# A weave that counts two more microseconds for each transfer, paces its reloads, and keeps two output weights on the chip

## The chip, the cores and the metric

The kernel runs on one core of a Trainium2 chip. The time is device time in microseconds (us), lower is better; three runs of the kernel before gave 2216.96, 2217.48 and 2220.29 us, a median of 2217.48.

## The reference

One inference step of a two-layer encoder for two groups of frames, 1024 of a prompt and 32 of a sample, 1024 wide, all in fp32. Cut to what matters:

```python
# layer 0: mLSTM mixer (8 heads, chunks of 64), layer 1: windowed attention (16 query heads, 2 kv heads)
mix = mlstm_mixer(x, w_in_a, b_gate_a, g_norm_a, w_out_a, C0, n0, m0)            # layer 0
x = layer_norm(ALPHA * x + mix, ln_g[0, 0], ln_b[0, 0])
x = layer_norm(ALPHA * x + swiglu(x, w_gu[0], w_down[0]), ln_g[0, 1], ln_b[0, 1])
k, v = split(x @ w_kv)
mix = sink_attention(x @ w_q_b, window(k), window(v), sinks, alibi) @ w_out_b    # layer 1
x = layer_norm(ALPHA * x + mix, ln_g[1, 0], ln_b[1, 0])
x = layer_norm(ALPHA * x + swiglu(x, w_gu[1], w_down[1]), ln_g[1, 1], ln_b[1, 1])
```

Outputs are x, the mLSTM states and the last key and value rows.

## The kernel before

**Tiling.** The 1056 frames of both groups are the columns of one activation ACT of 128 partitions by 8 tiles by 1056. A dense product is made of three fp32r matmuls (lines 677 to 679): the activation is held as a rounded high part and a low rest (SX), and so is each weight (tile w, two halves of 512 columns each). A weight read from its input goes through a raw tile wr: ScalarE makes the high part (line 429), VectorE or GpSimd the low part (line 443). ffn() uses a Strassen-like scheme of seven products; its intermediate results go out to DRAM (hs) and come back.

**Stages, by the time in the trace.** Projections and the mLSTM (0 to about 300 us; its small steps are woven between the projections' matmuls), output projection and norm (to 520), the first FFN (to 1205), the projections to k, v and q, attention and two quarters of its output projection (to 1450), the last two quarters woven with the norm (to 1560), the second FFN.

**Weights used more than once.** wkv, w_q_b and w_out_b serve three times each, since the frames come in three groups. The first time a weight is split it is written to DRAM in both parts, and later uses load the split halves (line 425, 512 KB each) from there. split_early() does this splitting ahead of its time, in quarters, beside the mLSTM: a quarter comes in to the tile area (line 1338), ScalarE casts it in place (line 1340), VectorE or GpSimd takes the rest (line 1342), and it goes out (line 1344). It ends when the flag early["over"] is set; what it has not reached is split at its first use.

**What sets the order.** The program is written out by a planner, Weave, while it is built. Each side task is a generator that yields At(engine, reads, writes): the engine of its next step and what that step needs. A Clock follows each instruction with estimated durations and keeps for each cell of each tile the time at which it is ready. Before and within each dense product, tick() places every side step whose estimated start has come. So the estimate decides only where a step stands in the queue of its engine; at run time every engine takes its queue in order, and a step whose operand has not landed holds all steps behind it. A transfer's end is estimated from a chain of all transfers, pipe, and 0.7 us.

**Halves.** Weights holds at most five halves in tiles w (SLOTS = 5). Its feed() asks for the next half as soon as a slot is free, or straight into a place given in home: the Mixer that opens after attention gives the tile E (ex in the trace) as home to weights 2 to 7 of the last use of w_out_b.

**The end of attention.** PLAN asks for the output tiles of the first quarters (g = 0 and g = 1) of w_out_b's eight weights among the q projections; late_out() then makes the last two quarters, g = 2 and g = 3, weights 0 to 7 in order, and reports each finished tile to norm_tail(), whose norms of the first quarters run meanwhile.

Of the kernel before, what the change touches and what calls it, by code (L numbers as in the profile page):

```python
# [19 lines left out]
KT = D // P  # L20
# [44 lines left out]
class Clock:  # L65
# [7 lines left out]
    def __init__(self, nc):  # L73
        self.nc = nc
        self.free = dict.fromkeys(self.LAG, 0.0)
        self.tiles, self.base = {}, {}
        self.lock, self.holder = 0.0, None
        self.pipe = 0.0
        self.window, self.busy, self.slow = -1, 0.0, True
        nc.push_inst_callback(self.see)  # L80

# [31 lines left out]
    def time(self, reads=(), writes=()):  # L113
# [6 lines left out]
                t = max(t, float(x[kinds, half, cells].max()))  # L120
        return t

    def begin(self, e, at):

        held = self.lock if self.holder != e else 0.0
        return max(self.free[e], at, held)
# [9 lines left out]
    def see(self, i, *_):  # L136
        e = str(i.engine).split(".")[-1]
        op = i.opcode
        if e not in self.free or op in ("EventSemaphore", "Drain", "UnconditionalBranch"):
            return  # L140
        aps = lambda l: [a for a in l if hasattr(a, "bass_ap")]
        inner = lambda l: [a for a in l if not a.bass_ap.tensor.name.startswith(("in_", "out_"))]
        ins, outs = aps(i.ins), aps(i.outs)
        if not outs and op != "LoadActFuncSet":
            return
        at = self.time(inner(ins), inner(outs))
        own = self.free[e] + 0.163 if e == "PE" else 0.0
        start = self.free[e] if at <= own else max(self.free[e], at + self.LAG[e])
        size = lambda a: int(np.prod([c for _, c in a.ap[1:]]))
        if op == "DMACopy":  # L150
            n, row = 4, min(a.ap[-1][1] * 4 for a in (*ins, *outs))
            for _, c in outs[0].ap:
                n *= c
            rate = 0.39 if row >= 2048 else 0.30 if row >= 1024 else 0.2 if row >= 512 else 0.1 if row > 4 else 8.5e-5
            self.pipe = max(start + 1.3, self.pipe) + n / rate / 1e6
            self.free[e] = start + 0.4
            end = self.pipe + 0.7
        elif e == "PE":
            end = self.matmul(i, start, size(ins[0])) + 0.163
        else:  # L160
            d = self.cost(i, e, op, ins, outs, size) / 1e3
            if len(outs) > 1 and e == "DVE":
                d += 0.08
            if e in ("DVE", "Pool") and self.shared(e, op, i, ins, outs):
                if self.holder not in (None, e):
                    start = max(start, self.lock)
                self.lock, self.holder = start + d, e
            end = start + d
            part = outs and outs[0].ap[0][1] in (HEADS, 64)
            self.free[e] = end + (0.014 if part else -self.LAP.get(e, 0.0))  # L170
        for l, kind in ((ins, 1), (outs, 0)):
            for a in inner(l):
                x, half, cells = self.part(a.bass_ap, a.ap)
                x[kind, half, cells] = end
# [45 lines left out]
class At:  # L220
# [7 lines left out]
    def start(self, clk):  # L228
        if self.time is None:
            if self.when and not self.when():  # L230
                return None
            reads = self.reads() if callable(self.reads) else self.reads
            self.time = clk.time(reads, self.writes)
        t = self.time
        for ring in self.room:
            if not ring.open():
                return None
            t = max(t, ring.time(clk))
        if t:
            t += clk.LAG.get(self.engine, 0.034)  # L240
        if self.engine is None:
            return t
        if self.engine == "EITHER":
            return min(clk.begin(e, t) for e in ("DVE", "Pool"))
        if self.engine == "SP":
            return max(t, clk.free["SP"], clk.pipe - 1.0)
        return t if self.engine == "PE" else max(t, clk.free[self.engine])
# [87 lines left out]
class Weights:  # L335
# [151 lines left out]
    def start(self, clk):  # L487
        if not (self.ahead and self._ready()):
            return None
        key = self.jobs[self.njob]  # L490
        t = clk.whole(self.raw[key[0]]) if key[0] in self.raw else 0.0
        if key in self.home:
            t = max(t, clk.time((), (self.home[key],)))
        else:
            t = max(t, self.new.ring("w").time(clk))
        return max(t + clk.LAG[self.engine], clk.free[self.engine])

    @property
# [17 lines left out]
def kernel(ctx: ExitStack, tc: tile.TileContext, A, O):  # L516
    nc = tc.nc
    ctx.enter_context(tc.manual_schedule())
    clk = Clock(nc)
# [38 lines left out]
    def add(name, idx):  # L558
        units.append(A[name][idx] if idx is not None else A[name])
        return len(units) - 1  # L560
# [19 lines left out]
    def again(name, m):  # L580

        u = add(name, m)
        if (name, m) in split:
            halves[u] = split[name, m]
        else:
            split[name, m] = kept[u] = dram.tile([P, 2, 2, D // 2], F32, name=f"{name}_{m}")
            first[name, m] = u
        return u
# [30 lines left out]
    U_B = {}  # L619
    for kind, m, g in PLAN:  # L620
        name, m0 = {"q": ("wqb", m), "k": ("wkv", 0), "v": ("wkv", 1), "o": ("wout_b", m)}[kind]
        U_B[kind, m, g] = again(name, m0)
    U_OUT_B = [again("wout_b", u) for u in range(8)]
    add_ffn(1)
    on_vector.update((u, 1) for u in U_OUT_A)
    on_vector.update((u, f) for u in U_Q[:1] + U_KV + [U_B['q', 0, 0]] for f in range(2))
# [5 lines left out]
    W = Weights(nc, clk, new_weight, units, pairs, on_vector, kept, halves, wv)  # L632
# [824 lines left out]
    lx = Mixer(ea.close, U_OUT_A[:6])  # L1457
# [429 lines left out]
    eb = ExitStack()  # L1887
# [244 lines left out]
    for kind, m, g in PLAN:  # L2132
        u = U_B[kind, m, g]
        if kind == "q":
            wv.until(lambda: ast["scored"] >= 3 * (done - 3))
            q_group(m, g)
            done += 1
        elif kind == "o":
            wv.until(lambda: ast["split"] > g and (not g or ast["scored"] >= min(53 + 3 * m, 72)))
            outs.append(out_tile(u, m, g, True))  # L2140
            W.done(u)
        else:
            for t in (1, 2):
                (k_group if kind == "k" else v_group)(u, t)
                if kind == "v":
                    wv.launch(v_turn(t))
            W.done(u)
            if kind == "v":
                v_parts(9, cv[:], P)
                k_part(ck, SEQ, P)  # L2150
                nc.sync.dma_start(O["p_k"], kout[:, :P])
                nc.sync.dma_start(O["s_k"], kout[:, P:])
                nc.sync.dma_start(O["p_v"], vT[2][:, 128:256])
                nc.sync.dma_start(O["s_v"], vT[2][:, 256:])
    wv.drain(task)
    wv.drain(parts)
    for t in outs:
        wv.drain(t)
    lx = Mixer(eb.close, U_OUT_B[2:])

    def late_out(g, cols, after):
        for m in range(KT):
            if g > 1:
                out_tile(U_OUT_B[m], m, g)
                if g == 3:
                    W.done(U_OUT_B[m])
            after(range(KT), m)

    tasks = norm_tail(2, late_out, [lx])
    ffn(1, 3, tasks, lx, True)  # L2170
# [127 lines left out]
```

## Time and profile before

| | us |
|---|---|
| median of three runs | 2217.48 |
| profiled execution, whole | 2219.07 |
| its span | 2217.3 |
| TensorE (PE) busy in it | 2182.8 |

Of the profiled execution 1.8 us lie around its span, and it is 1.6 us over the median of the three runs. Times in the trace count from the start of the span. "Idle" is time in which an engine does nothing that the profile shows; a releaser is whatever ended it. SPq stands for the DMA issues of SyncE.

### The profile page before, as it was taken

The page shows a single profiled execution, that of the slowest core. Times are in us where ns is not written, and L with a number is a line of the kernel's source. Part 1 is how long each engine was busy: PE and PEld are TensorE (multiplying, and loading weights), DVE is VectorE, ACT ScalarE, POOL GpSimd, SP SyncE. Part 2 cuts the span into 40 slices and gives each one's busy share as a digit, 9 for nine tenths or more (in the row PEclk, how much of TensorE's full clock was granted, in tenths as well). Part 3 has the DMA queues.
Part 4 walks back from the last instruction along what each step waited for, and adds up shares of the span by engine and source line. Part 5 has one row for each costly group of instructions (what it writes and reads, how often), then busy time and mean ns, then how long its engine had stood idle before and what let it go on. Part 6 is the DMA issues. An engine that isn't in the chain of part 4 may idle for free.

```text
span 2217.3 us, 44432 instructions
## 1 busy us (share of the span) xinstructions
PE 2182.8 (98%) x17116; PEld 2150.9 (97%) x17116; DVE 1512.6 (68%) x3030; ACT 1021.9 (46%) x2308; POOL 800.0 (36%) x805
## 2 busy tenths in 40 slices
PE   9999999999999999999999999999999999999997
PEld 9989999999999999999999999989999999999997
DVE  5566566777766566476677887778675665566677
ACT  4554454555434444321245877657443443421234
POOL 1343300001544545444401565500454554544510
PEclk9999999999999999999999999999999999999999
DMA  4455522302434424598516568761344344489712
GB/s 154 143 155 174 185 81 74 118 30 77 170 123 173 148 107 165 188 309 283 174 66 223 175 194 267 233 212 58 117 166 146 128 155 145 135 290 322 244 52 78
DMA packets 218052, 356.69 MB, mean 161 GB/s; under 512 B 18608, under 2 KB 151016, under 8 KB 217840
## 3 DMA queue, kind: packets, MB, share of 16 engines
q1 hardware_dynamic: 212800, 348.54, 47.0%
q10 hardware_dynamic: 5040, 5.31, 0.7%
q8 instruction: 135, 2.21, 0.4%
q14 instruction: 77, 0.63, 0.1%
HBM read 251.96 MB, written 101.82 MB: 160 GB/s over the span
## 4 chain that ended last, share of the span: by engine, by line
PE 85%; DVE 5%; DMA 4%; ACT 3%; issue 1%; SPq 1%; POOL 1%; ACTq 0%; DVEq 0%; POOLq 0%
PE d L677 10%; PE d L678 10%; PE d L679 10%; PE A L677 9%; PE A L679 9%; PE A L678 9%; PE B L677 7%; PE B L678 7%; PE B L679 7%; PE T L2068 1%; PE O L2085 1%; PE psS L2049 1%; PE O L2084 1%; PE psS L2050 1%; DMA wr<-in_dn 1%
## 5 line engine op out<-in xcount | busy, mean ns | idle before, releaser
L443 POOL TENSOR_TENSOR w<-wr,w 128x512 fp32r<-128x512 f32 x395 | 561.5, 1437 | 796.2 <-ACT w L429 793.5
L429 ACT CAST w<-wr 128x512 fp32r<-128x512 f32 (+1 forms) x478 | 290.3, 617 | 454.6 <-DVE wr L390 262.7
L677 PE MATMUL A<-sx,w 128*128 128x264 f32 x1280 | 364.1, 284 | 4.2 <-ACT z L1706 3.7
L679 PE MATMUL A<-sx,w 128*128 128x264 f32 x1280 | 363.4, 284 | 0.0
L678 PE MATMUL A<-sx,w 128*128 128x264 f32 x1280 | 363.1, 284 | 0.0
L677 PE MATMUL d<-sx,w 128*128 128x264 f32 (+2 forms) x1092 | 339.5, 311 | 3.3 <-DMA w<-wout_b 2.8
L678 PE MATMUL d<-sx,w 128*128 128x264 f32 (+2 forms) x1092 | 329.5, 302 | 1.5 <-DVE sx L800 1.5
L679 PE MATMUL d<-sx,w 128*128 128x264 f32 (+2 forms) x1092 | 329.3, 302 | 0.0
L677 PEld LDWEIGHTS A<-sx,w 128*128 128x128 f32 x1280 | 240.4, 188 | 5.1 <-ACT z L1706 4.1
L679 PEld LDWEIGHTS A<-sx,w 128*128 128x128 f32 x1280 | 241.2, 188 | 0.0
L678 PEld LDWEIGHTS A<-sx,w 128*128 128x128 f32 x1280 | 240.8, 188 | 0.0
L677 PE MATMUL B<-ex,w 128*128 128x264 f32 x832 | 236.6, 284 | 0.0
L679 PE MATMUL B<-ex,w 128*128 128x264 f32 x832 | 235.9, 284 | 0.0
L678 PE MATMUL B<-ex,w 128*128 128x264 f32 x832 | 235.9, 284 | 0.0
L677 PEld LDWEIGHTS d<-sx,w 128*128 128x128 f32 x1092 | 205.5, 188 | 5.3 <-DMA w<-wout_b 3.0
L678 PEld LDWEIGHTS d<-sx,w 128*128 128x128 f32 x1092 | 205.8, 188 | 2.6 <-DVE sx L800 2.1
L679 PEld LDWEIGHTS d<-sx,w 128*128 128x128 f32 x1092 | 205.4, 188 | 0.0
L677 PE MATMUL d<-sx,ex 128*128 128x264 f32 x552 | 160.3, 290 | 0.0
L1572 DVE TENSOR_TENSOR z<-z 128x528 fp32r<-128x528 f32 x136 | 110.3, 824 | 72.8 <-ACT z L1570 72.5
L679 PE MATMUL d<-sx,ex 128*128 128x264 f32 x552 | 156.7, 284 | 1.1 <-DVE ex L443 1.1
L679 PEld LDWEIGHTS B<-ex,w 128*128 128x128 f32 x832 | 156.8, 188 | 0.0
L678 PE MATMUL d<-sx,ex 128*128 128x264 f32 x552 | 156.7, 284 | 0.0
(303 smaller groups left out, 5858.2 us busy)
## 6 DMA issues: line engine op xcount, KB each, us to landing
wr<-in_gu SPq DMA_DIRECT2D x96, 512.0 KB, 4.8
hs_x<-z SPq DMA_DIRECT2D x72, 528.0 KB, 3.1
hs_t<-z SPq DMA_DIRECT2D x64, 528.0 KB, 3.5
sx<-hs_x SPq DMA_DIRECT2D x112, 264.0 KB, 5.6
w<-wqb SPq DMA_DIRECT2D x48, 512.0 KB, 4.4
sx<-hs_t SPq DMA_DIRECT2D x64, 264.0 KB, 6.0
ex<-hs_t SPq DMA_DIRECT2D x64, 264.0 KB, 6.0
w<-wout_b SPq DMA_DIRECT2D x33, 512.0 KB, 4.3
```

The costliest lines, as they stand in the source:

```text
L429: self.nc.scalar.copy(hi, r)
L443: eng.tensor_sub(lo, r, hi.bitcast(F32))
L677: nc.tensor.matmul(out, ah, bh, start=start and k == 0, stop=False, **kw)
L678: nc.tensor.matmul(out, ah, bl, start=False, stop=False, **kw)
L679: nc.tensor.matmul(out, al, bh, start=False, stop=stop and k == last, **kw)
L1572: clk.sooner(2 * N4, hi).tensor_sub(lo.bitcast(F32R), buf(s), hi)
L2049: nc.tensor.matmul(psS[h][:R, lo:256], q[:, h, tk], KH[g2][:, kc], start=True, stop=False)
L2050: nc.tensor.matmul(psS[h][:R, lo:256], q[:, h, tk], KL[g2][:, kc], start=False, stop=True)
L2068: nc.tensor.transpose(pt[:nk, i, h, :R], p[:R, h, c : c + nk], ident[:R, :R])
L2084: nc.tensor.matmul(po[:, :, :R], v, hi[:nk, i, :, :R], start=(i == 0), stop=False)
L2085: nc.tensor.matmul(po[:, :, :R], v, low[:nk, i, :, :R], start=False, stop=(i == len(kts) - 1))
```

## The change

Four edits, none of which changes what is computed.

- Clock keeps the set of all estimated ends of transfers, landing, and late() adds 2.0 us to a time that is one of them. A side step (At) and the cast of a raw weight count on that later time. The step waits at run time for the same things as ever; it only stands further back in the queue of its engine.
- A split half that SyncE loads is asked for no earlier than 1.3 us before the estimated end of the chain of transfers.
- The last uses of weights 6 and 7 of w_out_b are no longer weights of their own: U_OUT_B[6] and [7] are the ones of g = 1, and they are not given back after g = 1. The Mixer's tile E is home to weights 0 to 5.
- late_out() goes through the weights in the order 6, 7, 0 to 5.

```diff
@@ class Clock
         self.pipe = 0.0
+        self.landing = set()
...
+    def late(self, t):
+
+        return t + 2.0 if t in self.landing else t
...
             end = self.pipe + 0.7
+            self.landing.add(end)
@@ class At, start
-            self.time = clk.time(reads, self.writes)
+            self.time = clk.late(clk.time(reads, self.writes))
@@ class Weights, start
-        t = clk.whole(self.raw[key[0]]) if key[0] in self.raw else 0.0
+        t = clk.late(clk.whole(self.raw[key[0]])) if key[0] in self.raw else 0.0
...
             t = max(t, self.new.ring("w").time(clk))
+        if self.engine == "SP":
+            t = max(t, clk.pipe - 1.3)
         return max(t + clk.LAG[self.engine], clk.free[self.engine])
@@ units
-    U_OUT_B = [again("wout_b", u) for u in range(8)]
+    U_OUT_B = [again("wout_b", u) for u in range(6)] + [U_B["o", m, 1] for m in (6, 7)]
@@ output tiles among the q projections
             outs.append(out_tile(u, m, g, True))
-            W.done(u)
+            if u not in U_OUT_B:
+                W.done(u)
@@ late quarters
-    lx = Mixer(eb.close, U_OUT_B[2:])
+    lx = Mixer(eb.close, U_OUT_B[:6])

     def late_out(g, cols, after):
-        for m in range(KT):
+        order = [6, 7, *range(6)]
+        for i, m in enumerate(order):
             if g > 1:
                 out_tile(U_OUT_B[m], m, g)
                 if g == 3:
                     W.done(U_OUT_B[m])
-            after(range(KT), m)
+            after(order, i)
```

The program keeps all its TensorE instructions. split_early() gets through 15 weights where it got through 16, so that three weights of w_out_b, not two, are split at their first use; 33 loads of its halves into tiles w become 27, and as before 11 go to E.

**Place 1, SyncE's queue where the last halves are asked for.** A load's source names the weight: wout_b_0 to wout_b_7; act<-scrx brings back the residual. Line 425 of the kernel before is line 431 of the changed one. Before:

```order
L425 DMA w_1904_17817<-wout_b_7_82 128x2x512
L425 DMA w_1905_17819<-wout_b_0_75 128x2x512
L2121 DMA act_93<-scrx_95 128x288
L425 DMA w_1919_17894<-wout_b_0_75 128x2x512
L425 DMA w_1920_17896<-wout_b_1_76 128x2x512
...
L425 DMA w_1921_17928<-wout_b_1_76 128x2x512
L425 DMA w_1922_17930<-wout_b_2_77 128x2x512
L425 DMA ex_1923_17944<-wout_b_2_77 128x2x512
```

And changed:

```order
L431 DMA w_1902_17770<-wout_b_7_82 128x2x512
L2129 DMA act_93<-scrx_95 128x288 x2
L431 DMA w_1909_17821<-wout_b_7_82 128x2x512
L431 DMA w_1913_17840<-wout_b_0_75 128x2x512
L2129 DMA act_93<-scrx_95 128x288 x3
L431 DMA ex_1920_17926<-wout_b_0_75 128x2x512
L431 DMA ex_1920_17926<-wout_b_1_76 128x2x512 x2
```

Four halves between weight 7 and the first load to E have gone (five are now one).

**Place 2, TensorE's queue at the start of the late quarters.** The first row of each half of a weight is shown. Before, where weight 7 of g = 1 ends and weights 0, 1 and 2 follow:

```order
L677 MATMUL d_1918_17893<-sx_94,w_1904_17817 128x264
...
L677 MATMUL d_1925_17952<-sx_94,w_1905_17819 128x264
...
L677 MATMUL d_1925_17952<-sx_94,w_1919_17894 128x264
...
L677 MATMUL d_1927_17991<-sx_94,w_1920_17896 128x264
...
L677 MATMUL d_1927_17991<-sx_94,w_1921_17928 128x264
...
L737 MATMUL ln_1929_18014<-z_1924_17948,onesm_84 128x264
```

And changed, where weights 6, 7 and 0 follow:

```order
L685 MATMUL d_1919_17885<-sx_94,w_1909_17821 128x264
...
L685 MATMUL d_1922_17934<-sx_94,w_1895_17718 128x264
...
L685 MATMUL d_1922_17934<-sx_94,w_1899_17754 128x264
...
L685 MATMUL d_1923_17969<-sx_94,w_1902_17770 128x264
...
L685 MATMUL d_1923_17969<-sx_94,w_1909_17821 128x264
...
L745 MATMUL ln_1924_17988<-z_1921_17930,onesm_84 128x264
...
L685 MATMUL d_1927_18011<-sx_94,w_1913_17840 128x264
```

The four halves after weight 7 of g = 1 are now those that g = 1 used, and the norm's first sum (ln) still stands three matmuls into the fourth.

**Place 3, ScalarE's queue beside the mLSTM,** where it copies the first part of the projection qT of a pair of heads; nm is the decay matrix of an item of the mLSTM, junk its head norm, area the early split. Before:

```order
L1308 COPY act_93<-T_295_2093 128x128
L1340 CAST area_86_941<-area_86_941 128x256
L1206 ACTIVATE nm_282_2028<-nm_282_2028,cols2_204 128x128 x2
L1024 COPY qT_307_2136<-d_276_2002 128x384
L1278 ACTIVATE junk_311_2163,small_298_2103<-H_296_2096,small_298_2103 128x128 x2
```

And changed:

```order
L1316 COPY act_93<-T_279_2030 128x128
L1214 ACTIVATE nm_254_1898<-nm_254_1898,cols1_203 128x128 x2
L1032 COPY qT_287_2060<-d_263_1947 128x384
L1214 ACTIVATE nm_269_1967<-nm_269_1967,cols1_203 128x128 x2
L1348 CAST area_86_941<-area_86_941 128x256
L1286 ACTIVATE junk_300_2127,small_296_2108<-H_294_2101,small_296_2108 128x128 x2
```

The cast of the area stood ahead of the mLSTM's own steps and now stands behind two items' of them.

## The prediction

> **What bounds the kernel now.** I read the page's busy times first, then a table of stages, then the waits of TensorE, then the timelines around its longest waits.
>
> ```profile
> span 2217.3 us, 44432 instructions
> PE 2182.8 (98%) x17116; PEld 2150.9 (97%) x17116; DVE 1512.6 (68%) x3030; ACT 1021.9 (46%) x2308; POOL 800.0 (36%) x805
> ```
>
> TensorE (PE) is busy for 2182.8 of 2217.3 us. The change leaves its matmuls alone, so all that can move is the 34.5 us of idle time and the granted clock. Where the idle lies, by stage (the first number is the stretch, then PE's busy time, then those of its weight loads and of the other engines):
>
> ```profile
> 60.00:300.00 240.00, 234.61 (x1661) 217.08 (x1661) 151.38 (x592) 122.64 (x434) 87.90 (x196) 1.00 0.55 165
> 1205.00:1440.00 235.00, 233.32 (x1766) 229.33 (x1765) 187.08 (x690) 178.77 (x544) 133.07 (x180) 1.00 0.68 220
> 1440.00:1560.00 120.00, 113.37 (x900) 110.51 (x898) 98.50 (x177) 72.74 (x135) 6.09 (x6) 1.00 0.37 129
> 2200.00:2217.00 17.00, 5.59 (x32) 4.14 (x30) 11.03 (x21) 8.16 (x17) 1.39 (x2) 0.75 0.38 129
> ```
>
> Beside the mLSTM PE idles 240.00 - 234.61 = 5.4 us, beside attention 1.7, in the late quarters and the norm 6.6, in the last norm 11.4, which the change does not touch. So at most 13.7 us are within its reach. The waits of PE in the first and the third of these stretches (total, times, longest):
>
> ```profile
> PE T L1305 <- DVE ht L1299: 2.6, 5, 1.1
> PE T L1305 <- DVE ks L1225: 0.8, 1, 0.8
> PE T L1305 <- DVE Cn L1265: 0.6, 2, 0.3
> PE S L1216 <- DVE small L1292: 0.5, 1, 0.5
> PE S L1216 <- DVE p L1221: 0.4, 1, 0.4
> PE H L1239 <- DVE p L1221: 0.4, 1, 0.4
> PE d L677 <- DMA w<-wout_b: 2.8, 1, 2.8
> PE ln L737 <- DVE z L744: 1.8, 4, 0.7
> PE d L678 <- DVE sx L800: 1.5, 3, 1.0
> ```
>
> One wait for a reload of an output weight is the longest of them; beside the mLSTM there are eleven short ones, all for VectorE (DVE), 5.3 us together.
>
> **Part 1, the late quarters begin with weights that stay.** The timeline of SyncE, PE and VectorE around the 2.8 us:
>
> ```profile
> 1447.54 1.45 SPq L425 DMA_DIRECT2D w<-wout_b  x2
> 1449.04 5.01 SPq L425 DMA_DIRECT2D ex<-wout_b  x6
> 1452.36 0.28 PE L679 MATMUL d<-sx,w 128*128 128x264 f32 x1
> 1455.41 0.39 PE L677 MATMUL d<-sx,w 128*128 128x264 f32 x1 [2.76 <-DMA w<-wout_b]
> 1453.18 0.43 DVE L744 TENSOR_TENSOR z<-z 128x264 f32<-128x264 f32 x1
> 1456.52 0.71 DVE L752 TENSOR_TENSOR act<-ln,act 128x528 f32<-128x528 f32 x1 [2.90 <-PE ln L737]
> ```
>
> The order shows the half that was late: the second of weight 1 (place 1, w_1921), asked for at 1447.54, landed just before 1455.41, 7.8 us later. In the changed order PE finds there the four halves that it used for g = 1 (place 2), so this wait cannot occur: 2.8 us go. What is late next is the first load to E, the second half of weight 0. At 264 columns matmuls start 0.12 us apart (1452.36 and its like), so a half of 12 lasts 1.45 us, and five halves stand before its use: 1452.4 + 7.2 = 1459.6. SyncE reaches it after the last act<-scrx, at about 1447.5 (where it issued the late half before). That is 12 us, against 7.8 for the late half and 11.0 for the typical load to E:
>
> ```profile
> w<-wout_b SPq DMA_DIRECT2D x33, 512.0 KB, 4.3
> ex<-wout_b SPq DMA_DIRECT2D x11, 512.0 KB, 11.0
> area<-in_wqb SPq DMA_DIRECT2D x32, 128.0 KB, 2.6
> area<-in_wout_b SPq DMA_DIRECT2D x24, 128.0 KB, 2.3
> wr<-in_wout_b SPq DMA_DIRECT2D x2, 512.0 KB
> 1460.00:1465.00 5.00, 4.26 (x34) 4.02 (x33) 4.95 (x8) 2.02 (x4) 1.31 (x1) 1.00 1.05 397
> ```
>
> The four reloads that are gone are 2.1 MB, which at the 397 GB/s of the last row is 5.2 us of a DMA that is full there (share 1.05), so the loads to E land earlier than they did. That shortening is hidden behind PE's matmuls: worth nothing, and without that cover worth up to those 5.2 us as a safety.
>
> Does the norm take the 2.8 us back? VectorE had finished the norm's first operand by 1453.61 and then waited 2.90 us, because the ln matmul stands behind the waiting half in PE's queue. In the changed queue ln stands at the same distance, so the norm moves forward with PE; its own waits (1.8 + 1.5) stay. Value: -2.8; bounds: -3.5 if the 0.7 us of ln goes with it, -1.3 if the 1.5 us of sx grows by as much.
>
> **Part 2, steps that wait for a transfer stand further back.** Beside the mLSTM the other engines wait for transfers while later work stands behind:
>
> ```profile
> ACT area L1340 <- DMA area<-in_wqb: 23.2, 16, 3.9
> ACT area L1340 <- DMA area<-in_wout_b: 21.9, 15, 3.9
> POOL qwz L1200 <- DMA wib<-scrw: 36.5, 20, 4.5
> 152.50 0.41 ACT L1340 CAST area<-area 128x256 fp32r<-128x256 f32 x1 [1.89 <-DMA area<-in_wqb]
> 152.81 0.69 ACT L1206 ACTIVATE nm<-nm,cols 128x128 f32<-128x128 f32 x2
> 153.59 0.42 DVE L1221 TENSOR_TENSOR p<-S,nm 128x256 f32<-128x256 f32 x1 [1.44 <-issue]
> 154.45 0.42 DVE L1299 TENSOR_TENSOR ht<-H,small 128x256 f32<-128x256 f32 x1
> 154.93 0.44 PE L1305 MATMUL T<-ident,ht 128*128 128x128 f32 x2 [0.87 <-DVE ht L1299]
> 132.06 1.05 POOL L1200 TENSOR_TENSOR qwz<-qT,wib 64x128 f32<-64x128 f32 x2 [2.96 <-DMA wib<-scrw]
> 135.11 0.42 DVE L1221 TENSOR_TENSOR p<-S,nm 128x256 f32<-128x256 f32 x1 [1.91 <-POOL qz L1196]
> 136.71 0.44 PE L1305 MATMUL T<-ident,ht 128*128 128x128 f32 x2 [1.07 <-DVE ht L1299]
> ```
>
> ScalarE (ACT) spends 45 us in 31 waits for the area, 1.5 us each: less than the 2.0 by which the change holds such a step back. Read from 152.50 down, one of them is a wait of PE: ACT holds for the area, its decay nm follows late, VectorE's p late, ht behind p late, PE idles 0.87 us. Place 3 is this very place, and there the cast now stands behind nm. At 132.06 a late wib does the same through GpSimd, p and ht: 1.07 us. These two, 1.9 us, I count as gone. The other nine waits, 3.4 us, I could not follow to a transfer. Bounds: -5.3 if all of them go, +2.5 if the reordered steps meet as many new waits as the ht group now has. Value: -1.9, the two that I traced, since the rows show their cause.
>
> **Part 3, what the slower early split leaves over.** One weight more is split at its first use, beside attention: two casts, two subtractions, two stores, and one raw load for two half loads.
>
> ```profile
> L429 ACT CAST w<-wr 128x512 fp32r<-128x512 f32 (+1 forms) x478 | 290.3, 617 | 454.6 <-DVE wr L390 262.7
> L443 POOL TENSOR_TENSOR w<-wr,w 128x512 fp32r<-128x512 f32 x395 | 561.5, 1437 | 796.2 <-ACT w L429 793.5
> ```
>
> ACT gains 2 x 0.62 = 1.2 us of work in a stretch where it is busy 178.8 of 235 us, GpSimd (POOL) 2 x 1.44 = 2.9 of 133; both lie beside PE's 233. Cost 0; without that cover the 4.1 us.
>
> **Part 4, halves at a pace.** A paced load stands later in SyncE's queue, behind bias rows and residuals; behind it stand the same. PE has no wait for w beside attention now, so there is nothing to win but the 1.7 us of idle, all of it for other reasons; I take 0, bounds -1 and +2.8, one reload as late as the one above.
>
> **The clock.** PE's longest wait, 2.57 us before the first down projection, is in the second of these windows, and in the third the granted clock is half; the longest wait of place 2 lies across the last two:
>
> ```profile
> 945.43:948.84 3.41, 1.35 (x11) 1.35 (x12) 2.06 (x3) 2.53 (x5) 1.28 (x1) 1.00 1.06 334
> 948.84:952.25 3.41, 3.41 (x18) 3.41 (x17) 3.41 (x4) 0.79 (x2) 2.98 (x2) 0.50 0.39 143
> 1450.60:1454.01 3.41, 2.05 (x17) 1.83 (x16) 2.98 (x7) 0.00 (x0) 0.00 (x0) 1.00 0.82 240
> 1454.01:1457.42 3.41, 2.01 (x14) 1.91 (x14) 0.90 (x2) 0.08 (x1) 0.00 (x0) 1.00 1.03 390
> ```
>
> Busy 1.35 of 3.41 us was followed by half the clock, a loss of 3.41 / 2 = 1.7 us; busy 2.05 and 2.01 was not. So the wait that goes cost its 2.8 us and no clock. The wait at 945 stays, as its queue keeps its order, but may fall differently on the windows: 1.7 us either way. The Trainium skill (TensorE: Matmul & The Clock Gate, HAM oscillation — how this bites in real kernels) has it that gaps up to about 3.4 us do no harm; by that rule the 1.7 us would not hang on the change. The trace speaks against it, since 2.57 us was enough.
>
> **Sum.** -2.8 - 1.9 + 0 + 0 = -4.7 us: 2219.07 becomes 2214.4 for the profiled execution. That one stands 1.6 us over the median of the runs, about one clock loss; the difference carried to the median gives 2217.48 - 4.7 = 2212.8.
>
> **Rivals.**
>
> *Only the late quarters gain.* The waits beside the mLSTM are replaced by others of the same size, as steps held back by a fixed 2 us meet other neighbours. For it: five causes among eleven waits, and at place 3 the mLSTM stands an item further back. Against it: the two that I traced have one cause, which goes. 2217.48 - 2.8 = 2214.7.
>
> *The norm takes the gain.* VectorE is busy 98.5 of 120 us in the third stretch, and PE waits there for sx and ln; if the norm, not PE, sets the start of the FFN, part 1 gives nothing and part 2 its 1.9: 2215.6. Against it: the norm's own 2.90 us wait was for PE.
>
> *Paced halves arrive late: slower.* If pacing leaves a half less time before its use than it takes to land, PE waits in the middle of g = 1 or attention. Each costs what the late half cost, 2.8 us, and four of them give 2217.48 - 4.7 + 4 x 2.8 = 2224.0; from two on the gain is gone. It decides where a half is asked for less than 4.3 us (the usual landing) to 7.8 us (under a full DMA) ahead. For it: DMA share 0.68 over all of attention, and pacing gives up lead. Against it: SyncE's queue asks for as many halves in the same places, with fewer bytes ahead of them.
>
> *The change does not do what it says:* the +2.0 us is a shift of every such step alike, so queues keep their relative order and only the first edit to the weights counts; that is the first rival's number, and place 3 speaks against it.
>
> **Chances.** Forecast 0.47 (own range 2210 to 2214); only the late quarters 0.26; the norm 0.10; slower 0.10; the rest, 0.07, is a better outcome than the forecast (all eleven waits, 2209.4). About 0.2%, 4.4 us, is what a measurement here can tell from no change, so faster means under 2213.0. The forecast falls on both sides of that bound: 0.40 of its 0.47 and the 0.07 make faster 0.47; the first two rivals and the rest of the forecast make no change 0.43; slower 0.10. For 8 in 10 the range goes from 2209.0 (parts 1 and 2 at their lower bounds: -3.5 - 5.3 = -8.8, 2208.7, nearly) to 2217.5 (part 1 at -2.8 with part 2 at +2.5).
>
> **What would show it.** Right: no wait of PE for w<-wout_b or ex<-wout_b between 1440 and 1475; the 45 us of ACT's waits for area under 15; PE's waits for ht under 1.5 us. Wrong: PE idle beside the mLSTM still over 5 us (first rival), PE's waits for sx and ln over 4 us (second), any wait of PE for w<-wqb or w<-wout_b (third).

## The result

The changed kernel takes 2210.89 us (median of 7 runs, 2210.25 to 2215.07); the kernel before, run beside it, 2218.42 (7 runs, 2216.96 to 2220.29). The ratio is 0.9971, with a 95% interval of 0.9960 to 0.9982: 7.5 us faster by the medians, about 6.4 by the ratio, and the interval lies wholly under 1. Four of the seven runs lie between 2210.25 and 2210.89, three between 2213.64 and 2215.07; what parts the two groups is not shown, since the profile is of the lower one and the granted clock is 0.997 in runs of both. Here and below, three executions that took 0.4 ms or more longer than the others of their kernel (one with the pacing alone, two of the kernel before) are left out of the medians. The profiled execution took 2210.60 us, 8.5 less than that of before. The page of the changed kernel:

```profile
span 2208.8 us, 44411 instructions
PE 2180.9 (99%) x17116; PEld 2150.6 (97%) x17116; DVE 1524.6 (69%) x3020; ACT 1016.9 (46%) x2306; POOL 802.6 (36%) x813
```

As many matmuls as before, and idle time of 27.9 us in place of 34.5. The table of stages of the changed kernel (length, busy time of PE, PEld, DVE, ACT and POOL, granted clock, DMA share, GB/s):

```profile
60.00:300.00 240.00, 238.09 (x1691) 221.46 (x1689) 148.80 (x592) 121.62 (x434) 90.49 (x201) 1.00 0.52 159
940.00:1205.00 265.00, 263.98 (x2088) 262.84 (x2086) 189.07 (x302) 87.95 (x161) 83.14 (x64) 1.00 0.63 211
1205.00:1440.00 235.00, 232.31 (x1760) 227.91 (x1760) 184.65 (x692) 174.47 (x539) 131.66 (x178) 0.99 0.66 218
1440.00:1560.00 120.00, 115.49 (x919) 113.10 (x918) 97.59 (x172) 74.94 (x136) 12.22 (x10) 1.00 0.32 111
```

The one row of the kernel before that was not shown:

```profile
940.00:1205.00 265.00, 262.43 (x2080) 261.37 (x2079) 187.87 (x302) 81.62 (x148) 79.91 (x62) 0.99 0.64 209
```

PE's idle time (length less busy time) beside the mLSTM fell from 5.4 to 1.9 us, in the first FFN's second half from 2.6 to 1.0, in the late quarters from 6.6 to 4.5; beside attention it grew from 1.7 to 2.7. How the lead builds up is read from three matmuls that both programs have, each at the end of a wait. Before:

```profile
364.66 0.44 PE L677 MATMUL d<-sx,w 128*128 128x384 f32 x1 [0.50 <-ACT area L1428]
947.49 0.39 PE L677 MATMUL A<-sx,w 128*128 128x264 f32 x1 [2.57 <-ACT z L1706]
1463.86 0.68 PE L737 MATMUL ln<-z,onesm 128*128 128x264 f32 x2 [0.74 <-DVE z L744]
```

After:

```profile
360.40 0.44 PE L685 MATMUL d<-sx,w 128*128 128x384 f32 x1 [0.50 <-ACT area L1436]
941.23 0.39 PE L685 MATMUL A<-sx,w 128*128 128x264 f32 x1 [1.02 <-ACT z L1714]
1455.89 0.69 PE L745 MATMUL ln<-z,onesm 128*128 128x264 f32 x2 [0.76 <-DVE z L752]
```

The lead is 4.3 us behind the mLSTM (3.5 of it is the idle time of the table; where the other 0.8 lies is not shown), 6.3 at the first down projection, where the wait for z is 1.55 us shorter, and 8.0 at the first norm after attention. Between the last two lie three things. The 3.41 us at half clock after the wait at 947 are gone: matmuls started 0.22 us apart there in place of 0.12, so some 15 were started in a time for 28, about 1.5 us lost (the prediction's 1.7 is half of the window). A new wait beside attention costs 1.0 us of idle time net of other waits, and as much clock, 2.5 together. And the late half of 2.8 us is gone: 1.5 - 2.5 + 2.8 = 1.8, against 1.7 read.

PE's waits in the changed kernel (total, times, longest):

```profile
PE O L2093 <- DVE lo L2086: 2.5, 2, 2.3
PE ln L745 <- DVE z L752: 1.9, 4, 0.8
PE d L686 <- DVE sx L808: 1.4, 3, 0.9
PE T L1313 <- DVE ht L1307: 1.2, 2, 0.7
PE T L1313 <- DVE small L1267: 0.3, 1, 0.3
PE T L1313 <- DVE ks L1233: 0.2, 1, 0.2
```

ScalarE's and GpSimd's waits for the transfers beside the mLSTM:

```profile
ACT area L1348 <- DMA area<-in_wout_b: 6.8, 6, 2.4
ACT area L1348 <- DMA area<-in_wqb: 2.7, 3, 1.5
POOL qwz L1208 <- DMA wib<-scrw: 49.1, 22, 6.9
```

Eleven waits of PE beside the mLSTM became four, 1.7 us together. ScalarE's waits for the area fell from 45.1 us to 9.5; GpSimd's for wib did not fall (36.5 before, 49.1 now). No wait for a weight is left between 1205 and 1560. At the top stands a wait that was not there before. The timelines of ScalarE, VectorE and PE around it:

```profile
1257.85 0.58 ACT L2082 CAST hi<-T 128x512 fp32r<-128x512 f32 x1
1258.34 0.98 ACT L1944 ACTIVATE Q<-d 64x384 fp32r<-64x384 f32 x2
1259.35 1.12 DVE L1948 SCALAR_TENSOR_TENSOR Q<-d,Q 64x384 fp32r<-64x384 f32 x2 [0.54 <-ACT Q L1944]
1260.50 1.29 DVE L2086 TENSOR_TENSOR lo<-T,hi 128x512 fp32r<-128x512 f32 x2
1261.25 0.39 PE L2093 MATMUL O<-lo,VR 128*128 128x256 f32 x1 [2.32 <-DVE lo L2086]
```

The same moments as two stretches of the table of stages:

```profile
1258.33:1261.74 3.41, 1.09 (x10) 0.90 (x9) 2.81 (x7) 2.57 (x7) 0.46 (x1) 1.00 0.86 293
1261.74:1265.16 3.42, 3.42 (x18) 3.42 (x16) 3.08 (x14) 2.72 (x9) 1.37 (x2) 0.50 0.46 147
```

It is no transfer: a lo of the attention stands on VectorE behind a new query Q, which itself waits 0.54 us for ScalarE, while the hi that lo is taken from was ready at 1258.43. In PE's queue no projection stands between the matmul of that hi and the one of lo, and the next 3.4 us run at half clock.

### The profile page after: what moved, and what is told of

Read it like the earlier page. It is cut to its first block, busy times and chain, and to the rows that moved or that the text cites. A ratio compares the mean times of both kernels' runs of the same rounds, so it can differ in the third digit from the quotient of the medians.

```text
span 2208.8 us, 44411 instructions
## 1 busy us (share of the span) xinstructions
PE 2180.9 (99%) x17116; PEld 2150.6 (97%) x17116; DVE 1524.6 (69%) x3020; ACT 1016.9 (46%) x2306; POOL 802.6 (36%) x813
## 4 chain that ended last, share of the span: by engine, by line
PE 90%; DVE 4%; ACT 3%; DMA 2%; issue 1%; SPq 0%; POOL 0%; ACTq 0%; DVEq 0%
PE d L685 11%; PE d L686 10%; PE d L687 10%; PE A L685 10%; PE A L687 10%; PE A L686 10%; PE B L685 7%; PE B L686 7%; PE B L687 7%; PE T L2076 1%; PE O L2093 1%; PE O L2092 1%; PE psS L2057 1%; PE psS L2058 1%; DMA wr<-in_dn 1%
## 5 line engine op out<-in xcount | busy, mean ns | idle before, releaser
L449 POOL TENSOR_TENSOR w<-wr,w 128x512 fp32r<-128x512 f32 (+1 forms) x394 | 556.1, 1427 | 753.0 <-ACT w L435 749.2
L1580 DVE TENSOR_TENSOR z<-z 128x528 fp32r<-128x528 f32 x136 | 122.1, 916 | 91.3 <-ACT z L1578 91.3
```

What stands on the lines that cost most here:

```text
L449: eng.tensor_sub(lo, r, hi.bitcast(F32))
L1580: clk.sooner(2 * N4, hi).tensor_sub(lo.bitcast(F32R), buf(s), hi)
```

## The experiments

All times are medians; each ratio is to the kernel before in the same comparison, whose median moved between 2218.4 and 2220.7 us, so ratios and not microseconds are compared across groups (the whole change; the next four rows; the next four; the last three). Where two intervals overlap, the ratios do not show that the kernels differ.

| kernel | us | ratio | 95% interval |
|---|---|---|---|
| whole change | 2210.89 | 0.9971 | 0.9960 to 0.9982 |
| shift of 2.0 alone | 2214.11 | 0.9970 | 0.9958 to 0.9981 |
| pacing alone | 2227.07 | 1.0030 | 1.0021 to 1.0040 |
| weights alone | 2220.01 | 0.9993 | 0.9984 to 1.0002 |
| shift and weights | 2210.56 | 0.9954 | 0.9940 to 0.9967 |
| shift of steps only | 2213.59 | 0.9974 | 0.9963 to 0.9985 |
| shift of splits only | 2220.87 | 1.0008 | 0.9999 to 1.0018 |
| shift of 4.0 alone | 2209.67 | 0.9958 | 0.9944 to 0.9971 |
| whole, late quarters in old order | 2215.96 | 0.9983 | 0.9974 to 0.9992 |
| shift of 2.0 and pacing | 2216.16 | 0.9990 | 0.9981 to 0.9999 |
| shift of 4.0 and weights | 2210.50 | 0.9962 | 0.9950 to 0.9975 |
| whole with 4.0 | 2214.74 | 0.9977 | 0.9968 to 0.9986 |

**The shift alone.** The first edit by itself:

```diff
+    def late(self, t):
+        return t + 2.0 if t in self.landing else t
...
-            self.time = clk.time(reads, self.writes)
+            self.time = clk.late(clk.time(reads, self.writes))
...
-        t = clk.whole(self.raw[key[0]]) if key[0] in self.raw else 0.0
+        t = clk.late(clk.whole(self.raw[key[0]])) if key[0] in self.raw else 0.0
```

> Only the first edit: a step whose operand comes by a transfer is planned 2.0 us later; loads of halves are asked for as before, all eight output weights are loaded again. Theory (the shift alone takes away the mLSTM's waits): TensorE's idle time between 60 and 300 us falls from 5.4 us to 2.5 or less, ScalarE's waits for area from 45 us to under 15, the wait of 2.8 us for the late half at about 1455 stays: 3 to 3.5 us faster than the kernel before, ratio 0.9985. Rival (the pacing clears the DMA queues, and that lets the area land earlier): idle stays over 4.5 us, ratio 0.9995 to 1.0005. If the 2.3 us wait for lo at 1261 of the changed kernel comes with the shift, it shows here as well and takes back some 2 to 4 us.

0.9970, some 6.5 us: more than the 3 to 3.5 expected. Its stage beside the mLSTM:

```profile
60.00:300.00 240.00, 237.60 (x1686) 220.77 (x1685) 149.61 (x591) 121.16 (x433) 91.20 (x201) 1.00 0.53 158
```

ScalarE's and GpSimd's waits for the mLSTM's transfers, and PE's for a reload:

```profile
ACT area L1346 <- DMA area<-in_wout_b: 7.4, 6, 2.5
POOL qwz L1206 <- DMA wib<-scrw: 41.3, 22, 5.8
PE d L683 <- DMA w<-wout_b: 0.6, 1, 0.6
```

Idle 2.4 us, without any pacing: the rival falls. ScalarE's waits for the area are down as in the whole change, GpSimd's for wib are not (36.5 us before); that points to the area, though the shift moves the steps behind both. Against the expectation the wait for w from wout_b is 0.6 us, not 2.8, although the weights are loaded and used as before; more on that below. The wait for lo is 0.8 us here, so it does not come with the shift.

**The pacing alone.**

```diff
+        if self.engine == "SP":
+            t = max(t, clk.pipe - 1.3)
```

> Only the pacing of the loads of halves on SyncE's queue. Theory: nothing by itself, ratio 0.9990 to 1.0010; TensorE's idle time between 60 and 300 us stays at 5 us or more and the wait at 1455 stays near 2.8. Rival (pacing clears the queues for area and scrw): idle between 60 and 300 falls under 3.5 us and the time by 2 us or more. Second rival (paced halves arrive late): a wait of TensorE for a w that comes from wqb or wout_b between 1205 and 1440, 1 to 3 us each, ratio 1.0005 to 1.002.

1.0030: slower, by 6.4 us by the medians, beyond what any of the theories gave. PE's waits:

```profile
PE d L679 <- DMA w<-wout_b: 3.3, 2, 2.4
PE O L2087 <- DVE lo L2080: 2.5, 2, 2.3
PE d L679 <- DMA w<-wqb: 1.0, 1, 1.0
```

Its stage beside attention, and the second of its two windows at half clock:

```profile
1205.00:1440.00 235.00, 230.78 (x1722) 226.36 (x1721) 185.05 (x678) 175.78 (x532) 128.81 (x174) 0.99 0.66 211
1463.22:1466.63 3.41, 3.41 (x14) 3.00 (x13) 1.94 (x3) 1.78 (x3) 0.47 (x1) 0.50 1.05 403
```

Paced halves are late for PE in three places, the wait of 2.3 us for lo appears, and two windows at half clock follow the two longest waits. Its idle time beside the mLSTM, 7.6 us, is not the pacing's: the next kernel has the same without it.

**The weights alone.**

```diff
-    U_OUT_B = [again("wout_b", u) for u in range(8)]
+    U_OUT_B = [again("wout_b", u) for u in range(6)] + [U_B["o", m, 1] for m in (6, 7)]
...
-        for m in range(KT):
+        order = [6, 7, *range(6)]
+        for i, m in enumerate(order):
```

> Only the last two edits: output weights 6 and 7 stay from the second group, and the late quarters take 6 and 7 first. Theory: the wait of 2.8 us at 1455 is gone and the norm behind it moves forward with TensorE: 2.8 us faster, ratio 0.9987; the idle time between 60 and 300 us stays at 5.4. Rival (the norm takes the gain): TensorE's waits for sx and ln after 1455 grow from 3.3 us to over 5, ratio 1.0000. On the wait for z at 945: if it hangs on when the load of in_dn lands in that execution, it may be anything from 0 to 2.6 us here, though nothing ahead of it is changed; if it is the order's, it is 2.6 us with a window at half clock behind it as before.

0.9993, with an interval from -3.6 to +0.4 us: it holds both the 2.8 expected and nothing. Its stages:

```profile
60.00:300.00 240.00, 232.43 (x1645) 214.39 (x1644) 150.16 (x590) 121.26 (x428) 88.55 (x196) 1.00 0.54 162
1440.00:1560.00 120.00, 116.66 (x932) 114.22 (x931) 100.40 (x186) 73.97 (x141) 9.60 (x10) 1.00 0.36 121
```

PE's waits in the norm:

```profile
PE d L678 <- DVE sx L800: 1.4, 3, 1.0
PE ln L737 <- DVE z L744: 1.9, 4, 0.8
```

In its place the edit does what was expected: PE is busy 3.3 us more than before between 1440 and 1560, and the waits for sx and ln are the 3.3 us of before, so the norm does not take the gain. But the stretch ahead, where nothing was changed and every engine's queue holds the same instructions in the same order, idles 7.6 us here and 5.4 in the execution of before: such waits differ from one execution to the next.

**Shift and weights without pacing.** The changed kernel less the pacing:

```diff
-        if self.engine == "SP":
-            t = max(t, clk.pipe - 1.3)
```

> All but the pacing. Theory (the two gains add, pacing gives nothing): 6 to 6.5 us faster than the kernel before, ratio 0.9971, as the whole change; TensorE idle between 60 and 300 us 2.5 us or less, no wait for w from wout_b at 1455. Rival (pacing is a part of the gain): 2 us or more behind the whole change, ratio 0.9980 or above. If the wait for lo at 1261 comes with the pacing, it is absent here and the kernel is some 2 to 4 us ahead of the whole change, ratio 0.9955.

0.9954, the lowest ratio of all and the one expected if the wait for lo came with the pacing: 3.8 us ahead of the whole change by the ratios. The intervals overlap, so it is not shown to be faster, but pacing is no part of the gain. The longest wait for lo on PE's timeline, and on VectorE's the Q that stands ahead of the late lo in the whole change:

```profile
1270.19 0.38 PE L2091 MATMUL O<-lo,VR 128*128 128x256 f32 x1 [0.80 <-DVE lo L2084]
1260.73 1.12 DVE L1946 SCALAR_TENSOR_TENSOR Q<-d,Q 64x384 fp32r<-64x384 f32 x2 [0.17 <-ACT Q L1942]
```

Without the pacing the lo that is late in the whole change (the same one by its number in VectorE's queue) starts at 1256.21, ahead of this Q. The longest wait for lo is 0.8 us, no window follows it, and this profile has no window at half clock at all before the last norm.

**Which half of the shift.** Of the two places that call late(), one at a time: only the steps, and only the splits of raw weights.

```diff
@@ steps only
+            self.time = clk.late(clk.time(reads, self.writes))
@@ splits only
+        t = clk.late(clk.whole(self.raw[key[0]])) if key[0] in self.raw else 0.0
```

> The first edit for half of its places: only the steps that read a transferred operand stand 2.0 us later, the splits of raw weights are planned at the transfer's modelled end, as before. Theory (the mLSTM's area and decay steps make the gain): TensorE idle between 60 and 300 us at 2.5 us or less, as with the whole first edit (2.4), and 5 us or more of the 6.5 by which that one beat the kernel before. Rival (the splits make it, as weight loads share the engines with the mLSTM): idle there over 5 us, under 2 us of gain.

> The other half of the first edit: only the splits of raw weights are planned 2.0 us later. Theory: the mLSTM keeps its waits (idle between 60 and 300 us over 5 us) and the time is within 2 us of the kernel before; at 1455, where the whole first edit left 0.8 of the 2.9 us wait for w from wout_b, this half shows the 0.8 too, as it moves the split work that the load waits behind. Rival: idle between 60 and 300 falls to 2.5 us here, 5 us or more of gain.

0.9974 and 1.0008: the steps make the gain, the splits none. Up to 400 us the queues with the splits only are those of the kernel before, so this edit changes nothing beside the mLSTM. Beside the mLSTM the first idles 2.8 us (a little over the 2.5 expected), the second 6.7. The row of the second:

```profile
60.00:300.00 240.00, 233.31 (x1653) 215.85 (x1652) 152.24 (x590) 122.78 (x432) 87.37 (x196) 1.00 0.55 163
```

Its waits for the one of the two area loads (23.2 us before; for the other 20.5, 21.9 before):

```profile
ACT area L1346 <- DMA area<-in_wqb: 23.9, 16, 3.4
```

**A longer shift.** The first edit alone, with another number:

```diff
-        return t + 2.0 if t in self.landing else t
+        return t + 4.0 if t in self.landing else t
```

> The first edit alone with 4.0 us in place of 2.0. Theory (what counts is that the plan's lag covers the real one; once it does, more brings nothing): within 2 us of the 2214.1 us with 2.0, TensorE idle between 60 and 300 us still at 2.5 us or less. Rival (the gain grows with the lag, some waits being 3.9 us long): 2 us or more ahead of it. Second rival (steps held too far back are waited for themselves): 3 us or more behind it, with new waits of TensorE for ht or small.

2209.67, with five runs between 2209.34 and 2210.60. By the ratios (0.9958 and 0.9970) it is 2.7 us ahead of 2.0, which speaks for the rival, but the intervals overlap. The stage:

```profile
60.00:300.00 240.00, 239.64 (x1700) 223.25 (x1699) 150.20 (x586) 116.83 (x424) 90.61 (x197) 0.95 0.49 146
```

Idle is 0.4 us there: more lag does remove what 2.0 left. PE has no new wait for ht or small; only its waits for the area in the output projection that follows grow, from 0.5 to 1.2 us.

**The order of the late quarters.** The whole change, but with the quarters in the old order:

```diff
-        order = [6, 7, *range(6)]
-        for i, m in enumerate(order):
+        for m in range(KT):
```

> The whole change but its last edit: output weights 6 and 7 stay, the late quarters take 0 to 7 in the old order. Theory (the order turns the kept weights into cover for the first reload): a wait of TensorE for w or ex from wout_b of 1 to 3 us between 1440 and 1475 us, 2212 to 2214 us. Rival (two reloads fewer are enough, the order is idle): no such wait, 2210 to 2211 us as the whole change.

0.9983, 2215.96 us: 2.7 behind the whole change by the ratios, as expected, though the intervals overlap. PE's waits:

```profile
PE d L685 <- DMA ex<-wout_b: 3.3, 2, 2.6
```

Two stretches of the late quarters:

```profile
1445.13:1448.54 3.41, 0.83 (x7) 0.69 (x6) 3.20 (x6) 0.00 (x0) 0.00 (x0) 1.00 1.01 321
1448.55:1451.96 3.41, 3.41 (x18) 3.41 (x17) 0.77 (x2) 0.00 (x0) 0.00 (x0) 0.50 0.98 296
```

Since the list given to E now starts with weight 0, the first weight used has to come into E, and PE waits for it; a window at half clock follows, and a second one at 1530 after a wait of 2.0 us for sx. With this list the new order is what covers these loads; the old order with a list that starts at weight 2 was not run.

**Where the pacing costs.** The first and second edit without the weights; the shift of 4.0 with the weights and no pacing; the whole change with 4.0:

```diff
@@ shift and pacing: the edits to U_OUT_B and late_out are left out
@@ shift of 4.0 and weights: the edit to feed's pace is left out, and
-        return t + 2.0 if t in self.landing else t
+        return t + 4.0 if t in self.landing else t
@@ whole with 4.0: the last two lines alone
```

> The shift of 2.0 us and the pacing together, without the two edits to the output weights. Theory (paced halves of the output weights are late for the late quarters, and only the kept weights hide it): TensorE waits 2 to 4 us for w or ex from wout_b between 1440 and 1475, a window at half clock behind it, 2215 to 2218 us, which is 1 to 4 us behind the shift alone (2214.1). Rival (the shift of the splits covers the pacing): the wait there is under 1 us, as with the shift alone, 2211 to 2214 us.

> The shift with 4.0 us and the two edits to the output weights, no pacing. Theory (with 4.0 us the wait for wout_b at 1455 was gone already, so kept weights have nothing to win there): within 1 us of the 2209.7 us of the shift of 4.0 alone. Rival (two reloads fewer free the queue for others): 2 us or more ahead of it, under 2207.7.

> The whole change with 4.0 us in place of 2.0. Theory (what the pacing costs beside attention stays, the mLSTM's waits go to the end): the wait of 2.3 us for lo near 1260 with half a clock window behind it, TensorE idle between 60 and 300 us under 1 us, 2209 to 2211 us. Rival (the lo wait hangs on the shift of 2.0 alone): no wait for lo over 1 us, 2205 to 2208 us.

Shift and pacing: 2216.16 us, 0.9990 against 0.9970 for the shift alone. The total is as the theory had it, the place only in part: the waits for wout_b are 1.4 us in two for w and 0.9 in two for E, without a window behind them, and the long wait for lo is there with its window. With 4.0, the weights add nothing (0.9962 against 0.9958), as expected. The pacing costs 4.2 us there (2214.74 against 2210.50; the intervals overlap, but in this one comparison all eleven runs with it, from 2213.43, lie above all five without, up to 2213.30), where 2209 to 2211 was expected. PE's longest wait for reloads in the whole change with 4.0:

```profile
PE d L685 <- DMA w<-wqb: 3.3, 2, 2.5
```

Its stage beside attention:

```profile
1205.00:1440.00 235.00, 228.74 (x1734) 223.49 (x1733) 185.29 (x690) 174.77 (x537) 129.14 (x176) 1.00 0.68 220
```

Beside attention it idles 6.3 us; without the pacing that stretch is busy 232.83, an idle time of 2.2. A wait of 2.3 us for lo stands in all five kernels with the pacing, and in the kernels without it the longest wait for lo is 0.8. The window at half clock that was expected behind it is there in three of the five, and not here nor with the quarters in old order. Why pacing brings Q ahead of lo is argued, not shown: with halves asked for later, the planner may have fewer projections to place between the steps of the attention. PE's queue bears that out only in part: of its first 50 matmuls behind the point where the programs with and without pacing part, 18 are projections' against 24, of the first 200, 90 against 86.

**A shorter shift.** The first edit alone, with 1.0:

```diff
-        return t + 2.0 if t in self.landing else t
+        return t + 1.0 if t in self.landing else t
```

> The first edit alone with 1.0 us in place of 2.0. Theory (the plan must cover the real lateness; ScalarE's waits for area were 1.5 us each on the mean, up to 3.9): half of the gain of 2.0 us, TensorE idle between 60 and 300 us 3 to 5 us, 2215.5 to 2218 us. Rival (any reordering of these steps does it): idle under 2.6 us there and 2212 to 2215 us.

2223.68 us, ratio 1.0020. In this order the first two outputs, x of the two groups, are no longer the reference's, although the edit only moves steps in the queues; why, no run shows. So its whole time decides nothing. The mLSTM states and the rows of k and v are right; beside the mLSTM it idles 3.9 us, as the theory had it.

**The same stretch in all profiles.** Up to 390 us the programs of the first row below hold, as far as the profiles show, the same instructions in the same order on every engine, and so do those of the third and of the fourth. So what differs within a row comes from the execution, not from the program.

| lag of the steps | kernels | idle time of PE, 60 to 300 us |
|---|---|---|
| none | before, pacing, weights, splits only | 5.4, 7.6, 7.6, 6.7 |
| 1.0 | shift of 1.0 | 3.9 |
| 2.0 | the six with the shift of the steps | 1.8, 1.9, 2.4, 2.7, 2.8, 2.9 |
| 4.0 | the three with 4.0 | 0.4, 0.6, 1.2 |

The rows do not overlap: the lag of the steps is what takes the idle time away. The profile of before has the lowest value of its row; by the means, 6.8 and 2.4, the shift of 2.0 is worth 4.4 us here.

Two more stretches are measured between matmuls of one number in PE's queue, with the same work between them. Beside attention (from the 9408th to the 11038th) the eight kernels without pacing take 212.9 to 214.5 us, and the five with it 215.5 to 219.2, the whole change 215.8. So the pacing costs time there in every kernel that has it. In the late quarters (from there to the 11266th) the five kernels with kept weights and the new order all take 30.4 us. The seven without these edits take 31.0 to 33.7, before 33.4, so what the weights are worth, 0.6 to 3.3 us, hangs on how late the reload lands and whether a window at half clock follows. (With the quarters in old order the matmuls in this stretch are others.)

No kernel is shown to beat the changed one: the intervals of those at 0.9954 to 0.9962 overlap its own.

## Why the prediction was right, and where it was not

The forecast, 2212.8 us and faster, lies 1.9 us above the 2210.89, and the range held it (its upper end, 2217.5, is 2217.2 by the terms it is made of, which changes nothing here); as a difference it was -4.7 us against -7.5 by the medians and -6.4 by the ratio. Its steps stood up unequally, and that the total came so near is in part luck: 3 us of gain from a wait and a window that were priced at 0 stand against 2.5 us of loss beside attention, also priced at 0.

*Part 2 was mis-sized.* -1.9 us was counted for the steps behind a transfer; the lead behind the mLSTM is 4.3, the idle time fell by 3.5 (by 4.4 between the means of the profiles), and the shift alone is worth -6.5 us of the whole time. The step that failed is the choice to count only the two waits whose cause could be traced. Of the eleven, four are left in the changed kernel and three with the shift alone, so most of the others go too, followed to a transfer or not. One of the two causes given is in doubt: GpSimd waits for wib as long as ever, and the ht waits still fell, which points to the area on ScalarE; no run parts the two. The sign of its upper bound, reordered steps that meet new waits, did not occur beside the mLSTM. And "at most 13.7 us are within its reach" left out the first FFN, where 2.0 us of the lead and the window at half clock lie.

*Part 1 was right in its place.* The wait for w from wout_b is gone and the norm followed: its waits are 1.9 + 1.4 us, as before. As a price, 2.8 us is near the top of what was seen: this wait is not the same in every kernel that keeps the old order. With the old weights and no pacing it was 2.8 us before, 0.6 with the shift, and with the shift of the steps only:

```profile
PE d L683 <- DMA w<-wout_b: 1.8, 1, 1.8
```

With the shift of the splits only it was 0.2. SyncE's and PE's queues hold the same in the same order before and with the splits only, and again with the whole shift and with the steps only. So it is not their order that makes 2.8 and 0.2, or 0.6 and 1.8; what is left is the moment of landing, with the small differences in the other engines' queues.

The edits to the weights gained 0.6 us alone by the medians, with an interval that holds 2.8, and 3.5 on top of the shift, where the intervals overlap. That the first load to E has time to spare was right: no wait for it is left.

*Part 3, nothing for one weight less,* held: no wait for it in any row. The edit that causes it is the shift.

*Part 4, nothing for the pacing,* was wrong: alone it costs 6.4 us, beyond the bound of 2.8, with the shift of 4.0 and the weights 4.2, and by the ratios 4.4 on top of the shift and 3.8 in the whole change, the last with overlapping intervals. All four point the same way. The third rival named one mechanism, halves asked for too late, and it is seen where PE waits for a w. The prediction missed the second: a pace also changes what stands ahead of what in the attention, and a wait of VectorE's order, 2.3 us, comes with it, in three kernels of five with a window at half clock. The profiles with and without pacing have the same span of 2208.8, but their programs are the same up to 1200 us, and there the one with pacing was 1.1 us ahead by nothing but the execution; this it lost again.

*The clock.* "The wait at 945 stays, as its queue keeps its order" failed: it went from 2.57 to 1.02 us, and its window with it, 3.1 us together. The order of the loads of in_dn was indeed the same. VectorE waited for them 6.7 us before, 5.2 after, 6.1 with the weights alone and 4.8 with the pacing alone, whose program is not shifted; so it varies between executions. PE's wait itself is 0.6 to 2.6 us in the four kernels without the shift of the steps, with a window in two, and 1.0 to 1.6 in the nine with it, with none. These overlap, so the gain of 3.1 us cannot be credited to the change.

*The rivals.* "Only the late quarters gain" falls by the first experiment, "the norm takes the gain" by the waits for ln and sx. Of the three signs named for a right forecast (no wait for wout_b, area under 15 us, ht under 1.5) all came: none, 9.5 and 1.2.

## What to carry to other kernels

Where a planner writes the queues, a step that depends on a transfer can be placed later than the planner's own estimate says: two microseconds of lag were worth more than the waits of the matmul engine that could be traced to a transfer, and four took away nearly all of them. Such an order has to be tried by its results too, as the lag of one microsecond shows. A wait for a transfer in one profile is one draw: look at a second profile of the same stretch, or of a kernel that does not touch it, before it is priced. Asking for loads later is an edit to the order of everything behind them, and has to be timed by itself, since the gain of the edits beside it can hide its cost.

## What the runs showed of the hardware

**A wait costs the clock by what share of a fixed window it fills.** Ahead of the last norm the windows at half clock are all 3.41 us long and lie on a grid of that length that runs through an execution. In this part of the profiles of before, of the change and of all experiments but the shift of 1.0, every window in which PE was busy 1.56 us or less was followed by one at half clock (0.83, 1.00, 1.09, 1.27, 1.35, 1.35, 1.42, 1.47, 1.49 and 1.56 us); between 1.57 and 1.70 both happen; from 1.81 on it never does. Two pairs that show both sides, first the shift alone, then the weights alone:

```profile
1955.20:1958.61 3.41, 1.56 (x13) 1.35 (x12) 2.06 (x4) 1.38 (x3) 0.68 (x1) 1.00 1.10 360
1958.64:1962.05 3.41, 3.41 (x17) 3.41 (x17) 3.41 (x4) 1.91 (x4) 1.87 (x3) 0.50 0.79 257
```

```profile
1964.80:1968.21 3.41, 1.65 (x14) 1.44 (x12) 2.36 (x4) 0.86 (x2) 0.66 (x2) 1.00 1.10 361
1968.21:1971.62 3.41, 3.09 (x25) 3.09 (x26) 3.11 (x3) 2.46 (x5) 2.61 (x3) 1.00 0.92 299
```

So a wait of some 2 us costs about 1.5 us more or nothing, by where it falls: the same wait of 2.3 us for lo has a window behind it in the whole change, where it left PE busy 1.09 us of one window, and none with the quarters in old order, where it left 2.32 and 2.09 of two. The Trainium skill (TensorE: Matmul & The Clock Gate, What's actually happening) describes a free-running window of 3413 ns; the grid agrees. The Trainium skill has the gate close after an idle window (the same section), and elsewhere (HAM oscillation — how this bites in real kernels) gives the rule that there be no idle gap over about 3.4 us, which the prediction read as: shorter ones do no harm. Here the runs disagree with that reading, since a window that was busy 1.56 of 3.41 us was enough.

**A granted clock that moved no time.** With the shift of 4.0 alone the clock stands at 0.95 through the profile up to the last norm, yet the first FFN is as long as with the full one (shift of 4.0 first, the changed kernel second):

```profile
520.00:940.00 420.00, 418.81 (x3447) 418.56 (x3446) 274.36 (x311) 173.03 (x311) 201.61 (x140) 0.95 0.43 149
```

```profile
520.00:940.00 420.00, 418.81 (x3446) 418.56 (x3444) 271.47 (x311) 171.72 (x311) 200.90 (x140) 1.00 0.43 149
```

As many matmuls in as much time: whatever that number records, PE did not run 5% slower.
